# A hybrid encoder block: branch A's attention result split by halves of the tokens, and a third buffer for gate copies

## The chip, the cores and the metric

The kernel runs on one core of one Trainium2 chip. The metric is the device time of one execution in microseconds, as the median of several runs. Beside the runs there is one profiled execution, whose trace gives each instruction's start and length on the five engines: PE (TensorE, with its weight loads as PEld), DVE (VectorE), ACT (ScalarE), POOL (GpSimd) and SP (SyncE), which here issues the transfers (SPq).

## The reference, cut to what matters

The block takes x (1024 tokens of 1024 numbers, with 16 learned tokens put ahead), normalizes it, and projects it to the inputs of two attention branches and to two gates. Each branch gives 512 numbers for each token. They are merged, and a feed-forward part follows:

```python
y_a = differential_attention(...)        # 1024 x 512
y_b = windowed_gqa(...)                  # 1024 x 512
merged = sigmoid(ga) * (y_a @ w_ba) + sigmoid(gb) * (y_b @ w_bb)
h = h + merged @ w_o
h = h + (silu(n @ w_gate) * (n @ w_up)) @ w_down     # n = rms_norm(h, norm_ffn)
return rms_norm(h, norm_final)
```

All is in float32. [...] Making the two parts is called a split here: ACT copies the high part (`split`, L111), and DVE or POOL subtracts it from the number to get the low part (L112).

## The kernel before, in words

The work is laid out with features on the 128 partitions and tokens along the row. After the projections and branch B's attention comes branch A's attention; the projections to the gates (`gate_steps`, L535) are put between its matmuls, to fill PE. A gate's product of 512 tokens takes 24 matmuls into one PSUM bank; ACT copies the bank to a buffer `gate_stage` (L539), of which there are G_BUFS = 2, and SP sends the buffer to a tensor g_d in DRAM (L540). Two PSUM banks serve these products. The attention results go to DRAM too: yb_d, and ya_d (L653, one transfer for each head and each half of the tokens).

The merge (L755 to L811) has two loops. Both use weights in eight columns of 128 output features: `branch_w` (L522) loads one column (256 KB) and splits it, on ACT and POOL, into `wbhb` (branch B) or `wbha` (branch A), with WB_BUFS = 5 buffers for both. `branch_mm` (L529) makes the product of one column and one half of the tokens (512): 4 chunks of 128 features by three matmuls, so 12 matmuls into one of eight PSUM banks. A pass of `gated` (L775) loads the gate's half row (`gt`, L778, GT_BUFS = 4 buffers), takes its sigmoid on ACT (L779), and calls `branch_mm`.

- Branch B's loop (L786): for each column and half, DVE multiplies gate and product into `tb` (L790). Its operand `yb` is loaded from yb_d in four transfers of 512 KB ahead of the loop and split in eight pieces of 512 tokens on ACT and DVE (`load_y`, L760). The raw numbers lie in a part of `tb` that is not yet in use, and the weights of the first two columns as well.
- Branch A's loop (L801): the same with `ya`, whose pool is opened where `yb`'s was closed (L791, L792), so in the same memory. DVE multiplies (L805), POOL adds `tb` (L806), and the sum is split into `mT` on ACT and DVE (L807). From the ninth pass on, a chunk of w_out is loaded and split in each pass (`prep_wo`, L749). The order of the passes is (column, half): columns 0 to 3 with both halves each, then columns 4 to 7 with the first half, then with the second.

The matmuls that follow (`po`, L832) multiply `mT` by w_out: four blocks of 128 tokens at a time, the first half of the tokens first.

The raw numbers of `ya`, of the weights and of w_out lie in a ring of RING_RAW = 5 buffers of 4 KB per partition (`raw_tile`, L744). The order of PE's instructions is that of the program text in this part (L784). Those of the other engines and of SP are put in order by a scheduler when the kernel is built; each engine and SP then works through its list strictly in order, and an instruction that waits holds up all behind it. Pools that are closed give their memory to pools opened later; an instruction that writes such memory waits until its last use is over.

`mpool` (L795), opened after `yapool`, holds `mT`, the row of norm_ffn (`gffn`, L797) and the first weights of the feed-forward part (`first_f`, L798 and L871).

## Time and profile before

| | us |
|---|---|
| median of 3 runs | 1466.54 |
| lowest and highest run | 1465.86, 1470.17 |
| the profiled execution's own time | 1467.45 |
| its span, first to last instruction | 1465.7 |
| mean granted TensorE clock in it (share of full speed) | 0.997 |

A line of the timeline gives the start and the length in us, the engine, the line of the kernel, the operation, what it writes <- what it reads, and the count of instructions merged; in brackets stands the idle time of the engine just before it, and what ended that. A line of the view of waits gives engine, tile and line <- what it waited for: us in total, times, and the longest. A line of the view of windows gives from:to, the length, the busy time of the engines asked for, then the granted clock, the share of the 16 transfer engines that was busy, and GB/s. A line on a tile's instructions gives the count, then min/median/max in ns. A line on transfers gives the count, the size of one, and the median us from issue to landing.

### The profile page before, as it was taken

What the parts mean: (1) busy time and instruction counts of PE and PEld (TensorE: products, weight loads), DVE (VectorE), ACT (ScalarE), POOL (GpSimd) and SP (SyncE); (2) the same over time, 40 slices, a digit from 0 to 9 for tenths busy, and PEclk for the clock granted to TensorE, in tenths of its full rate; (3) what the DMA queues carried; (4) which work ended last, traced back from release to release, by engine and by line L of the source; (5) the groups of instructions that cost most, each with busy time, mean ns of one, the idle gap of its engine ahead of it and who ended that gap; (6) DMA issues with size and microseconds to landing.
All of it is one profiled execution on the core that took longest, in us unless ns stands there. A gap on an engine that the chain in (4) does not pass through costs nothing.

```text
span 1465.7 us, 21002 instructions
## 1 busy us (share of the span) xinstructions
PE 1439.6 (98%) x7353; PEld 1237.5 (84%) x7353; DVE 859.0 (59%) x1664; ACT 654.6 (45%) x1237; POOL 529.8 (36%) x502
## 2 busy tenths in 40 slices
PE   6999999999999999999999999999999999999998
PEld 6988989988898989877888878888888888888886
DVE  6356426528686868423613876555555554787667
ACT  5365436525455555445412744333333333444454
POOL 4143223313323232223822566454545442000444
PEclk9999999999999999999999999999999999999999
DMA  7334353272524251086531434333333323954443
GB/s 233 89 98 115 111 127 98 77 204 96 152 73 145 73 153 66 31 277 196 169 126 61 141 122 135 126 103 98 108 103 105 101 93 102 345 201 141 125 124 142
DMA packets 155577, 189.96 MB, mean 130 GB/s; under 512 B 16128, under 2 KB 101568, under 8 KB 155472
## 3 DMA queue, kind: packets, MB, share of 16 engines
q1 hardware_dynamic: 155472, 188.63, 40.9%
q8 instruction: 58, 0.95, 0.3%
q14 instruction: 47, 0.39, 0.1%
HBM read 128.09 MB, written 53.94 MB: 124 GB/s over the span
## 4 chain that ended last, share of the span: by engine, by line
PE 86%; POOL 4%; issue 4%; DMA 3%; ACT 1%; DVE 1%; SPq 1%; POOLq 0%; ACTq 0%; DVEq 0%
PE pg L1055 26%; PE pp_g L199 10%; PE pd L1149 8%; PE ppa L532 6%; PE po L832 6%; PE aps L588 4%; PE apy L630 3%; PE pp_va L199 3%; PE pp_qb L199 3%; PE pp_qa L199 3%; PE pp_ka L199 3%; POOL oa L112 3%; PE apt L617 2%; PE bpt L337 2%; PE bpy L343 2%
## 5 line engine op out<-in xcount | busy, mean ns | idle before, releaser
L1055 PE MATMUL pg<-t,wop 128*128 128x512 f32 x1056 | 242.9, 389 | 0.2 <-POOL wop L112 0.2
L1055 PEld LDWEIGHTS pg<-t,wop 128*128 128x128 f32 x1056 | 198.1, 188 | 41.7 <-POOL wop L112 0.6
L112 POOL TENSOR_TENSOR wop<-wf,wop 128x512 fp32r<-128x512 f32 x128 | 171.6, 1345 | 165.9 <-ACT wop L111 152.1
L1149 PE MATMUL pd<-ob,oa 128*128 128x512 f32 x924 | 210.2, 389 | 0.8 <-POOL oa L112 0.4
L1149 PEld LDWEIGHTS pd<-ob,oa 128*128 128x128 f32 x924 | 173.3, 188 | 37.6 <-POOL oa L112 0.8
L1055 PE MATMUL pg<-b,wop 128*128 128x512 f32 x792 | 184.0, 390 | 2.7 <-DVE c L1064 2.7
L1055 PEld LDWEIGHTS pg<-b,wop 128*128 128x128 f32 x792 | 148.3, 188 | 34.2 <-issue 2.4
L112 POOL TENSOR_TENSOR wl_c<-w_c,wh_c 128x1024 fp32r<-128x1024 f32 x31 | 74.9, 2418 | 155.2 <-ACT wh_c L111 144.8
L111 ACT ACTIVATE wop<-wf 128x512 fp32r<-128x512 f32 x128 | 80.2, 631 | 85.2 <-PE pg L1055 48.4
L599 ACT ACTIVATE as<-as,amn 128x1040 f32<-128x1040 f32 x64 | 74.5, 1165 | 72.7 <-DVE amn L594 72.7
L112 POOL TENSOR_TENSOR oa<-ra,oa 128x512 fp32r<-128x512 f32 x33 | 44.0, 1335 | 170.8 <-ACT oa L111 169.4
L199 PE MATMUL pp_g<-hT_hi,wh_c 128*128 128x512 f32 x256 | 101.4, 396 | 0.6 <-DMA g_d<-gate_stage 0.6
L199 PE MATMUL pp_g<-hT_hi,wl_c 128*128 128x512 f32 x256 | 100.9, 394 | 0.0
L199 PE MATMUL pp_g<-hT_lo,wh_c 128*128 128x512 f32 x256 | 100.9, 394 | 0.0
L111 ACT ACTIVATE oa<-ra 128x512 fp32r<-128x512 f32 x77 | 48.7, 632 | 107.7 <-PE pd L1149 50.2
L588 PE MATMUL aps<-ak,aq 128*128 128x352 f32 (+1 forms) x384 | 92.6, 326 | 0.0
L832 PE MATMUL po<-woh,mT 128*128 128x512 f32 x384 | 88.0, 390 | 0.0
L890 DVE TENSOR_TENSOR s<-wf,wf 128x512 f32<-128x512 f32 x22 | 26.8, 1217 | 103.9 <-DMA wf<-in_w_ff_gate_dram 56.2
L832 PEld LDWEIGHTS po<-woh,mT 128*128 128x128 f32 x384 | 71.9, 188 | 14.8
L588 PEld LDWEIGHTS aps<-ak,aq 128*128 128x128 f32 x384 | 69.6, 188 | 14.0
L594 DVE CUSTOM_DVE_ANT_0 as<-aps,dist,amn 128x352 f32<-128x352 f32 (+1 forms) x128 | 71.3, 564 | 10.4 <-PE aps L588 8.4
L324 POOL TENSOR_SCALAR bs<-bs,bdn 128x432 f32<-128x432 f32 (+1 forms) x64 | 37.0, 596 | 94.8 <-DVE bdn L322 81.4
(249 smaller groups left out, 2943.1 us busy)
## 6 DMA issues: line engine op xcount, KB each, us to landing
ra<-aop SPq DMA_DIRECT2D x77, 256.0 KB, 2.6
w_c<-in_w_in_dram SPq DMA_DIRECT2D x33, 512.0 KB, 4.0
wf<-in_w_ff_gate_dram SPq DMA_DIRECT2D x24, 512.0 KB, 3.8
wf<-in_w_ff_up_dram SPq DMA_DIRECT2D x24, 512.0 KB, 3.8
aop<-as SPq DMA_DIRECT2D x44, 256.0 KB, 2.1
aop<-c SPq DMA_DIRECT2D x33, 256.0 KB, 2.0
g_d<-gate_stage SPq DMA_DIRECT2D x32, 256.0 KB, 2.0
gt<-g_d SPq DMA_DIRECT2D x32, 256.0 KB, 3.4
```

Source lines behind the costliest of these rows:

```text
L111: nc.scalar.activation(hi, src, AF.Copy)
L112: lo_eng.tensor_tensor(lo, src, f32(hi), ALU.subtract)
L199: nc.tensor.matmul(ps[:, :n], a[:, c, :], b[:, c, at:at + n], start=(c == 0 and i == 0), stop=(c == DC - 1 and i == 2))
L324: nc.gpsimd.tensor_scalar(st[:, r, :W], st[:, r, :W], dn[:, r:r + 1], 1.0, ALU.mult, ALU.mult)
L532: nc.tensor.matmul(ps, w[:, a, j, :], src[j][:, b, tk], start=(j == 0 and n == 0), stop=(j == 3 and n == 2))
L588: nc.tensor.matmul(ps[:, :n], qs[m][:, t * P:(t + 1) * P], ks[m][:, vv, k0:k0 + n], start=(vv == 0), stop=(vv == 1))
L594: nc.vector.tensor_tensor_reduce(s[m][:, a:b], ps[:, a - k0:b - k0], far_by, slope, low, ALU.add, ALU.min, mn[:, m, i + j:i + j + 1])
L599: nc.scalar.activation(s[m][:, 0:L], s[m][:, 0:L], AF.Exp, bias=low, scale=-1.0, accum_out=dn[:, m:m + 1])
L630: nc.tensor.matmul(py[:, cols], v[:kp, a, k, :], at_[:kp, k, b, :], start=(k == 0 and j == 0), stop=(k == 8))
L832: nc.tensor.matmul(ps, mT[:, c, a, t * P:(t + 1) * P], wos[q, c][:, b], start=(c == 0 and n == 0), stop=(c == DC - 1 and n == 2))
L1055: nc.tensor.matmul(ps, op[:, x, c, :], b[:, y, c, :], start=(p in (1, 2, 5) and c == 0 and n == 0), stop=(p in (4, 2, 3) and c == 3 and n ...
L1149: nc.tensor.matmul(ps[u], oa[:, a, u * P:(u + 1) * P], ob[:, b, :], start=(p in (1, 2, 5) and j == 0 and k == 0), stop=(p in (2, 3, 4) and ...
```

## The change

Branch A's `ya` is no longer loaded as four tensors of 1024 tokens after branch B's loop. It is loaded and split by halves of the tokens. A half has four loads of 512 tokens (256 KB each) into two ring buffers (`load_ya`) and four splits on ACT and DVE (`split_ya`). The first half is loaded after branch B's second column, and one of its pieces is split in each of the passes of B's columns 2 to 5, into a pool of its own (`ya0pool`, 16 KB per partition) that is opened ahead of `ybpool`. The second half is loaded after B's sixth column and split into `yapool` once `ybpool` is closed. Branch A's passes are put in the order columns 0 to 3 with the first half, then with the second, then columns 4 to 7 likewise. `yb` is loaded as before, written out in place. G_BUFS goes from 2 to 3.

```diff
-G_BUFS = 2
+G_BUFS = 3
...
-                nc.tensor.matmul(ps, w[:, a, j, :], src[j][:, b, tk],
+                nc.tensor.matmul(ps, w[:, a, j, :], src(j, b, tk),
...
     tb = ypool.tile([P, DC, S], F32, name="tb")
+    ya0pool, close_ya0 = pool("ya0pool")
     ybpool, close_yb = pool("ybpool")
...
+    def load_ya(half):
+        for i in range(2):
+            raw_ya[half, i] = raw_tile(f"raw_ya{half}_{i}")
+            for k in range(2):
+                nc.sync.dma_start(raw_ya[half, i][:, k * 512:k * 512 + 512], ya_d[2 * i + k][:, half * 512:half * 512 + 512])
+
+    def split_ya(half, j, p):
+        ya_t[half, j] = p.tile([P, 2, 512], F32R, name=f"ya{half}_{j}")
+        split(ya_t[half, j][:, 0], ya_t[half, j][:, 1], raw_ya[half, j // 2][:, j % 2 * 512:j % 2 * 512 + 512], nc.vector)
+
+    def ya(j, b, tk):
+        return ya_t[tk.start // 512, j][:, b]
...
             nc.vector.tensor_tensor(tb[:, o, tk], gt, ps, ALU.mult)
+        if o in (1, 5):
+            load_ya(o // 4)
+        if 2 <= o < 6:
+            split_ya(0, o - 2, ya0pool)
     close_yb()
     yapool, close_ya = pool("yapool")
-    ya = load_y(yapool, ya_d, "ya", lambda j: raw_tile(f"raw_ya{j}"))
+    for j in range(4):
+        split_ya(1, j, yapool)
...
-    order_a = [(o, h) for o in range(4) for h in range(2)] + [(o, h) for h in range(2) for o in range(4, DC)]
+    order_a = [(o, h) for b in range(0, DC, 4) for h in range(2) for o in range(b, b + 4)]
...
     close_ya()
+    close_ya0()
     close_ypool()
```

More of the change, by code (lines that the diff above doesn't have):

```diff
@@ L755, in encoder_block, with yb @@
     tb = ypool.tile([P, DC, S], F32, name="tb")
+    ya0pool, close_ya0 = pool("ya0pool")
     ybpool, close_yb = pool("ybpool")
     first_w = [branch_w(ypool, o, w_bb, "b", tb[:, 2, o * 512:o * 512 + 512]) for o in range(2)]
-    def load_y(p, src, nme, raw_of):
-        ys, raws_y = [], []
-        for j in range(4):
-            raws_y.append(raw_of(j))
-            nc.sync.dma_start(raws_y[j], src[j])
-            ys.append(p.tile([P, 2, S], F32R, name=f"{nme}{j}"))
-            if j % 2:
-                for h in range(2):
-                    cols = slice(h * 512, h * 512 + 512)
-                    for k in (j - 1, j):
-                        split(ys[k][:, 0, cols], ys[k][:, 1, cols], raws_y[k][:, cols], nc.vector)
-        return ys
-    yb = load_y(ybpool, yb_d, "yb", lambda j: tb[:, 4 + j, :])
+    yb_t = []
+    for j in range(4):
+        nc.sync.dma_start(tb[:, 4 + j, :], yb_d[j])
+        yb_t.append(ybpool.tile([P, 2, S], F32R, name=f"yb{j}"))
+        if j % 2:
+            for h in range(2):
+                cols = slice(h * 512, h * 512 + 512)
+                for k in (j - 1, j):
+                    split(yb_t[k][:, 0, cols], yb_t[k][:, 1, cols], tb[:, 4 + k, cols], nc.vector)
+    def yb(j, b, tk):
+        return yb_t[j][:, b, tk]
+    ya_t, raw_ya = {}, {}
+    def load_ya(half):
[8 more added lines that the diff above has]
+        return ya_t[tk.start // 512, j][:, b]
     def gated(i, o, half, w, src):
@@ L790, in encoder_block @@
             nc.vector.tensor_tensor(tb[:, o, tk], gt, ps, ALU.mult)
+        if o in (1, 5):
+            load_ya(o // 4)
+        if 2 <= o < 6:
+            split_ya(0, o - 2, ya0pool)
     close_yb()
     yapool, close_ya = pool("yapool")
-    ya = load_y(yapool, ya_d, "ya", lambda j: raw_tile(f"raw_ya{j}"))
+    for j in range(4):
+        split_ya(1, j, yapool)
     mpool, close_mpool = pool("mpool", "right")
```

## Prediction

> **What bounds the kernel now.** I read the page first: which engine is full, and whose time the chain of work that ended last holds.

> ```profile
> PE 1439.6 (98%) x7353; PEld 1237.5 (84%) x7353; DVE 859.0 (59%) x1664; ACT 654.6 (45%) x1237; POOL 529.8 (36%) x502
> PE 86%; POOL 4%; issue 4%; DMA 3%; ACT 1%; DVE 1%; SPq 1%; POOLq 0%; ACTq 0%; DVEq 0%
> ```

> TensorE (PE) is busy 98% of the span. The change takes no matmul away, so it can gain only where PE stands still or runs slowly. The view of PE's waits gives the places:

> ```profile
> PE pg L1055 <- DVE c L1064: 2.7, 2, 2.0
> ...
> PE ppa L532 <- ACT ya L111: 1.7, 1, 1.7
> ...
> PE pp_g L199 <- DMA g_d<-gate_stage: 0.6, 1, 0.6
> PE ppa L532 <- DVE ya L112: 0.5, 2, 0.3
> PE ppa L532 <- DVE yb L112: 0.4, 2, 0.2
> ```

> The change touches the ya waits (the step from branch B's products to branch A's) and the gate_stage wait. The timeline of PE shows the first place:

> ```profile
> 641.54 41.55 PE L532 MATMUL ppa<-yb,wbhb 128*128 128x512 f32 x182 [0.23 <-DVE yb L112]
> 684.75 0.50 PE L532 MATMUL ppa<-ya,wbha 128*128 128x512 f32 x1 [1.66 <-ACT ya L111]
> 685.48 2.15 PE L532 MATMUL ppa<-ya,wbha 128*128 128x512 f32 x6 [0.22 <-DVE ya L112]
> 687.88 4.35 PE L532 MATMUL ppa<-ya,wbha 128*128 128x512 f32 x14 [0.26 <-DVE ya L112]
> ...
> L532 PE MATMUL ppa<-yb,wbhb x192: 388/389/499, 638.2 to 682.7; 128*128 128x512 f32 x192
> ...
> 730.84 9.46 PE L832 MATMUL po<-woh,mT 128*128 128x512 f32 x41
> ```

> PE runs out of branch B's work at 683.09 and gets A's piece by piece. The cause is in ACT and DVE at the same moment:

> ```profile
> 684.09 4.26 ACT L111 ACTIVATE ya<-raw_ya 128x512 fp32r<-128x512 f32 x8
> 684.73 4.91 DVE L112 TENSOR_TENSOR ya<-raw_ya,ya 128x512 fp32r<-128x512 f32 x8 [0.84 <-ACT ya L111]
> ```

> All eight splits of ya start only when B's last product is done, since ya lies in yb's space. And the windows, one microsecond each (PE busy, granted clock, DMA share, GB/s), show that PE pays twice:

> ```profile
> 685.00:686.00 1.00, 0.78 (x3) 1.00 0.80 242
> 686.00:687.00 1.00, 1.00 (x5) 0.72 0.88 263
> 687.00:688.00 1.00, 0.74 (x3) 0.50 0.85 279
> 688.00:689.00 1.00, 1.00 (x3) 0.50 0.84 258
> 689.00:690.00 1.00, 1.00 (x4) 0.58 0.86 256
> 690.00:691.00 1.00, 1.00 (x6) 1.00 0.69 178
> ```

> After the wait the clock is halved for about 3.4 us: 0.28 + 0.50 + 0.50 + 0.42 = 1.70 us lost beside the idle time.

> **Part 1: half of ya is ready before B ends.** B's 182 matmuls take 41.55 us. One lasts 0.39 (the median of 389 ns in the row above) and they overlap, so the spacing is (41.55 - 0.39)/181 = 0.2274 us. Without a wait A's first matmul starts at 641.54 + 182 x 0.2274 = 682.93, its 192 matmuls take 43.66, and the first po matmul comes at 726.59 instead of 730.84: **4.25 us**. The other way round: waits of 1.66 + 0.22 + 0.26 = 2.14, three broken overlaps of 0.39 - 0.23 = 0.16 each, and 1.70 of clock make 4.32. I take 4.25.

> What has to be ready in time? The first four A products use the first half's ya alone. It is split on ACT and DVE beside B's products, some 34 us before use. The second half's splits still wait for the end of B (about 683.1). By the changed program's order of instructions ACT has two gate sigmoids and a w_out split ahead of them; if those run to 685.4, the four ACT and four DVE splits end at about 685.4 + 4 x 0.53 + 0.8 = 688.3 (0.53 = 4.26/8, 0.61 = 4.91/8 for DVE, from the rows above). They are first needed after 48 matmuls, at 682.93 + 10.92 = 693.85. Slack 5.5 us, so cost nothing; with the cover gone it would be the same kind of wait as today's.

> **Part 2: what moves ahead in SP's and ACT's queues.** The four first-half loads of ya (256 KB each) take the place of branch B's weight loads for columns 2 to 4 in SP's order, and four ya splits stand before these weights' splits on ACT. This is the change's own danger, for PE asks for column 2 early in B.

> ```profile
> 638.35 2.08 SPq L524 DMA_DIRECT2D wbrb<-in_w_branch_b_dram  x3
> ...
> 642.15 1.33 SPq L524 DMA_DIRECT2D wbrb<-in_w_branch_b_dram  x2
> ...
> wbrb<-in_w_branch_b_dram SPq DMA_DIRECT2D x2, 256.0 KB, 4.9
> ...
> DMA to landing us min/median/max: 8.0/8.7/10.3
> ...
> 643.06 2.19 ACT L779 ACTIVATE gt<-gt 128x512 f32<-128x512 f32 x4
> ...
> 645.86 5.05 POOL L112 TENSOR_TENSOR wbhb<-wbrb,wbhb 128x512 fp32r<-128x512 f32 x4 [11.17 <-ACT wbhb L111]
> ```

> (The line of landings is that of the four 512 KB loads of raw_ya; the wbrb line that of the two loads issued from 642.15 on.) Three ya loads go out at 638.35; the fourth after the last gate copy at 642.15; column 2's weights at about 642.8. The position in the transfers is that of today's fifth wbrb, which landed after 4.9 us, so 647.7. ACT finishes four gates at 645.25, the fourth ya split (its load lands at about 647.0) by 647.6, column 2's high half at 648.3; POOL's low half takes 5.05/4 = 1.26, to 649.6. PE wants the high half after 48 matmuls of B, at 641.54 + 38 x 0.2274 = 650.18, the low half two matmuls later, 650.64. Slack about 1.0 us: **cost taken as 0**, since the nearest row by place and size is the 4.9. The bounds: nothing can be gained here (today PE does not wait for wbhb); with the slowest ya landing, 10.3, POOL ends at 655.0 and PE waits 4.4, with a halved clock after it 6.1. Columns 3 and 4 follow at POOL's 1.26 against 5.5 us of PE each.

> **Part 3: what moves into branch A's time.** norm_ffn's row and the two first weights of the feed-forward part (three transfers of 512 KB) move on SP from B's time to behind A's third gate load. The order of A's products becomes four columns by first half, then by second. A gate buffer comes free after multiply, add and split:

> ```profile
> L805 DVE TENSOR_TENSOR gt<-gt,ppa x16: 672/686/689, 690.2 to 734.8; 128x512 f32<-128x512 f32 x16
> L806 POOL TENSOR_TENSOR gt<-gt,tb x16: 1283/1292/1747, 691.0 to 735.7; 128x512 f32<-128x512 f32 x16
> L111 ACT ACTIVATE mT<-gt x16: 614/616/634, 693.8 to 737.3; 128x512 fp32r<-128x512 f32 x16
> L112 DVE TENSOR_TENSOR mT<-gt,mT x16: 686/1139/1676, 694.5 to 738.0; 128x512 fp32r<-128x512 f32 x16
> DMA to landing us min/median/max: 2.5/3.4/9.4
> ...
> 690.00:732.00 42.00, 42.00 (x187) 34.75 (x186) 25.05 (x28) 19.93 (x35) 36.27 (x26) 1.00 0.54 165
> ```

> 0.69 + 1.29 + 0.62 + 1.14 + 3.4 (gt's landing) + 0.63 (its sigmoid, alike) = 7.8 us, against four products of 12 x 0.2274 = 10.9 us per buffer; and eight PSUM banks let PE run eight products (21.8 us) ahead of a late multiply. The DMA share of 0.54 at 165 GB/s would become about 0.66 with 1.5 MB more in 42 us. So 0, and at most one late gate of 9.4 in place of 3.4 us, which the banks cover. POOL's 36.27 us are no more than before. po asks first for first-half tokens; A's last four products are second-half ones in both orders, so no new wait there. From po on, the order on every engine is that of before, so an earlier start is carried to the end.

> One more thing on Part 2. mT's low half takes DVE 686 to 1676 ns beside POOL, ya's 4.91/8 = 0.61 us with POOL idle; if one new ya split held POOL up for 0.61 us, column 2 would still keep 0.4 of its slack. [...]

> **Part 4: the third gate copy buffer.**

> ```profile
> 320.60 0.57 ACT L539 COPY gate_stage<-pp_g 128x512 f32<-128x512 f32 x1
> 331.79 0.58 ACT L539 COPY gate_stage<-pp_g 128x512 f32<-128x512 f32 x1 [10.62 <-DMA g_d<-gate_stage]
> ...
> 332.42 0.50 PE L199 MATMUL pp_g<-hT_hi,wh_c 128*128 128x512 f32 x1 [0.59 <-DMA g_d<-gate_stage]
> ```

> The third copy waits for the first one's transfer, which stands behind the attention loads, and PE then waits for a bank. With three buffers the third copy needs no transfer: **0.6 us**. The fourth waits to about 331.8 instead, when its bank isn't yet wanted. All later copies cost PE nothing today.

> **Sum.** 4.25 + 0.6 = 4.85 us off the profiled execution's own 1467.45 (span 1465.7 and 1.75 around it): **1462.6**. That execution lies 0.9 over the runs' median of 1466.54, whose runs go from 1465.86 to 1470.17. By the trace alone I cannot say that each run has the halved clock; a run without it would be at 1467.45 - 1.70 = 1465.75, about the lowest one. The changed kernel should have none, so I set its median a little under the sum: **1462.4**, 4.1 us or 0.28% under the median.

> **The rivals.**
> - *Late weights (the slower side).* Column 2's weights land after more than 5.9 us (648.7) and PE waits in B at 650. For: the DMA queue is full there and the slack is 1.0. Against: the row of 4.9. A landing of 7 us gives a wait of about 1 and 1463.6; the slowest landing gives 1462.6 + 6.1 = 1468.7. It ends above the median from a wait of 2.2 with the halved clock (3.9 together), a landing of about 8.1.
> - *The halved clock is not due to the wait and stays.* Then only 2.14 + 0.48 + 0.6 = 3.2 goes: 1464.2. For: the wait of 1.99 us for c is followed by no drop:

> ```profile
> 855.46 5.72 PE L1055 MATMUL pg<-b,wop 128*128 128x512 f32 x24 [1.99 <-DVE c L1064]
> ...
> 853.00:856.00 3.00, 1.01 (x6) 1.00 0.33 116
> 856.00:859.00 3.00, 3.00 (x15) 1.00 0.02 5
> ```

>   Against: that wait stood alone, ours has two more behind it, and the drop begins 1.7 us after its end (0.72 in the window from 686). [...]
> - *The split does not do it.* The second half, a weight or a gate is late inside A and PE waits at 693.9 instead: a wait of 2.1 with the clock gives the 4.25 back and leaves 1466.8.

> **Chances.** Faster by over 0.3% means under 1462.1, slower over 1470.9 (0.3%, 4.4 us, is about what a measurement of this kernel can tell from no change). Forecast 0.72: its own range 1461.2 to 1463.8 lies across 1462.1, because the median may or may not hold the halved clock, so 0.42 faster, 0.30 same. Late weights 0.14: 0.10 same, 0.04 slower, where columns 3 and 4 are late as well. Clock stays 0.08, same. Split does not do it 0.06: 0.05 same, 0.01 slower. Sum: **faster 0.42, same 0.53, slower 0.05**. Range 1460.5 to 1467.0: it takes in the late weights up to a wait of about 3 and the rival of the clock, and leaves out under 2 in 10.

> **What would show it.** Right: no PE wait for ya, first po matmul 48 us less 4.25 after B's end, no window under 1.00 there, ya's first splits on ACT between 645 and 648, no wait at pp_g near 332. Wrong: PE waiting for wbhb near 650, or for ya, wbha or a PSUM bank after 683; or the same clock drop without a wait.

## The result, and the profile after

| kernel | median, us | lowest to highest | runs | ratio to before [95% interval] |
|---|---|---|---|---|
| before | 1467.28 | 1465.72 to 1471.44 | 19 | |
| changed | 1464.08 | 1461.67 to 1468.95 | 19 | 0.9979 [0.9971, 0.9988] |
| changed, measured again beside experiments | 1465.80 | 1463.82 to 1468.37 | 11 | 0.9992 [0.9983, 1.0001] |

The change is worth 0.1 to 0.2%, some 1.5 to 3 us: under the 0.3% that counts as a difference here, and less than the 4.1 us of the forecast. The interval of the second measurement takes in 1, no change. The profiled execution of the changed kernel takes 1464.08 (span 1462.3) against 1467.45 (span 1465.7).

The waits of PE in the changed kernel: engine, tile and line <- what it waited for, us in total, times, longest.

```profile
PE pg L1076 <- DVE c L1085: 2.3, 2, 2.0
...
PE apt L617 <- DVE as L605: 0.7, 1, 0.7
PE ppa L532 <- POOL wbha L112: 0.7, 1, 0.7
```

The waits for ya, yb and the gate copy are gone. Two of 0.7 us are new: for the first softmax of branch A (`apt`, its transposes, <- `as`), and for a low half of branch A's weights (`wbha` <- POOL). PE's timeline of the merge:

```profile
638.60 43.75 PE L532 MATMUL ppa<-yb,wbhb 128*128 128x512 f32 x192
682.19 30.54 PE L532 MATMUL ppa<-ya,wbha 128*128 128x512 f32 x134
713.43 13.44 PE L532 MATMUL ppa<-ya,wbha 128*128 128x512 f32 x58 [0.70 <-POOL wbha L112]
726.71 33.48 PE L853 MATMUL po<-woh,mT 128*128 128x512 f32 x147
```

Counted from start to start, before against after:

| stretch | before | after | difference |
|---|---|---|---|
| start of branch B's products | 638.16 | 638.60 | +0.44 |
| branch B's products, to A's first | 682.93 - 638.16 = 44.77, without the ya wait | 43.59 | -1.18 |
| branch A's products and the waits ahead of and in them, to po | 730.84 - 682.93 = 47.91 | 44.52 | -3.39 |
| first po | 730.84 | 726.71 | -4.13 |

The -3.39 is the forecast 4.25 less the new wait of 0.70 and its broken overlap of 0.16. The -1.18 was not forecast at all. And 0.7 us of the 4.13 is lost later: a stretch at half clock costs 1.7, and by the two views of waits some 1.0 of shorter ones in the feed-forward part comes back. In windows of the changed kernel (PE's busy time, granted clock, DMA share, GB/s):

```profile
687.00:690.00 3.00, 3.00 (x15) 1.00 1.08 318
...
851.00:854.00 3.00, 3.00 (x8) 0.54 0.02 5
854.00:857.00 3.00, 3.00 (x14) 0.89 0.24 90
```

After B's end the clock stays at 1.00. But now it is halved behind the wait for `c` in the feed-forward part, near 850, where it was not in the profile of before.

### The profile page after: what moved, and what is told of

Same layout as the page of the kernel before. It is cut to its first block, busy times and chain, and to the rows that moved or that the text cites. A ratio compares the mean times of both kernels' runs of the same rounds, so it can differ in the third digit from the quotient of the medians.

```text
span 1462.3 us, 21013 instructions
## 1 busy us (share of the span) xinstructions
PE 1438.5 (98%) x7353; PEld 1238.7 (85%) x7353; DVE 854.0 (58%) x1664; ACT 656.2 (45%) x1237; POOL 532.1 (36%) x502
## 4 chain that ended last, share of the span: by engine, by line
PE 88%; POOL 4%; issue 4%; DVE 2%; DMA 2%; ACT 0%; SPq 0%; POOLq 0%; DVEq 0%; ACTq 0%
PE pg L1076 28%; PE pp_g L199 12%; PE pd L1170 8%; PE po L853 6%; PE aps L588 4%; PE ppa L532 4%; PE apy L630 3%; PE pp_qb L199 3%; PE pp_ka L199 3%; PE pp_va L199 3%; PE pp_qa L199 3%; POOL oa L112 3%; PE apt L617 2%; PE bpt L337 2%; PE bpy L343 2%
## 5 line engine op out<-in xcount | busy, mean ns | idle before, releaser
L112 POOL TENSOR_TENSOR wop<-wf,wop 128x512 fp32r<-128x512 f32 x128 | 173.6, 1360 | 164.6 <-ACT wop L111 150.8
L112 POOL TENSOR_TENSOR wl_c<-w_c,wh_c 128x1024 fp32r<-128x1024 f32 x31 | 74.9, 2417 | 155.1 <-ACT wh_c L111 144.8
L111 ACT ACTIVATE wop<-wf 128x512 fp32r<-128x512 f32 x128 | 80.3, 632 | 85.2 <-PE pg L1076 50.7
L599 ACT ACTIVATE as<-as,amn 128x1040 f32<-128x1040 f32 x64 | 74.5, 1165 | 72.8 <-DVE amn L594 72.8
L112 POOL TENSOR_TENSOR oa<-ra,oa 128x512 fp32r<-128x512 f32 x33 | 44.0, 1335 | 170.5 <-ACT oa L111 169.1
L199 PE MATMUL pp_g<-hT_hi,wh_c 128*128 128x512 f32 x256 | 101.3, 396 | 0.0
L199 PE MATMUL pp_g<-hT_lo,wh_c 128*128 128x512 f32 x256 | 100.9, 394 | 0.0
L199 PE MATMUL pp_g<-hT_hi,wl_c 128*128 128x512 f32 x256 | 100.9, 394 | 0.0
L111 ACT ACTIVATE oa<-ra 128x512 fp32r<-128x512 f32 x77 | 48.7, 632 | 107.3 <-PE pd L1170 50.3
L911 DVE TENSOR_TENSOR s<-wf,wf 128x512 f32<-128x512 f32 x22 | 18.7, 850 | 107.0 <-DMA wf<-in_w_ff_up_dram 52.6
## 6 DMA issues: line engine op xcount, KB each, us to landing
ra<-aop SPq DMA_DIRECT2D x77, 256.0 KB, 2.6
aop<-as SPq DMA_DIRECT2D x44, 256.0 KB, 2.1
aop<-c SPq DMA_DIRECT2D x33, 256.0 KB, 2.0
g_d<-gate_stage SPq DMA_DIRECT2D x32, 256.0 KB, 2.0
gt<-g_d SPq DMA_DIRECT2D x32, 256.0 KB, 3.3
```

What stands on the lines that cost most here:

```text
L111: nc.scalar.activation(hi, src, AF.Copy)
L112: lo_eng.tensor_tensor(lo, src, f32(hi), ALU.subtract)
L199: nc.tensor.matmul(ps[:, :n], a[:, c, :], b[:, c, at:at + n], start=(c == 0 and i == 0), stop=(c == DC - 1 and i == 2))
L599: nc.scalar.activation(s[m][:, 0:L], s[m][:, 0:L], AF.Exp, bias=low, scale=-1.0, accum_out=dn[:, m:m + 1])
```

## The experiments

Ten measurements of nine kernels, in three sets; the kernels of a set shared a chip and the runs of before. The first set is the third buffer alone, the split alone, the low halves on DVE and the splits after B's end; the second is the changed kernel again, the split alone a second time, the low halves on DVE with two buffers, and `yb` moved; the third is the old order and both halves early. Medians are best compared within a set.

| experiment | median, us | lowest to highest | ratio to before [95% interval] |
|---|---|---|---|
| third buffer alone | 1467.19 | 1464.21 to 1471.19 | 0.9999 [0.9987, 1.0012] |
| split alone | 1466.07 | 1462.59 to 1468.36 | 0.9993 [0.9982, 1.0003] |
| split alone, second time | 1466.39 | 1465.09 to 1468.14 | 0.9992 [0.9984, 1.0001] |
| changed, low weight halves on DVE | 1464.06 | 1462.96 to 1465.60 | 0.9977 [0.9967, 0.9986] |
| the same, two gate buffers | 1463.64 | 1462.97 to 1467.85 | 0.9978 [0.9969, 0.9987] |
| changed, splits after B's end | 1474.07 | 1472.05 to 1474.69 | 1.0040 [1.0026, 1.0054] |
| changed, old order of A's passes | 1466.14 | 1463.44 to 1469.41 | 0.9994 [0.9982, 1.0005] |
| changed, both halves of ya early | 1466.78 | 1464.36 to 1469.03 | 0.9992 [0.9983, 1.0002] |
| before, with yb moved | 1467.05 | 1465.56 to 1470.25 | 0.9997 [0.9988, 1.0007] |

### The third gate buffer alone

```diff
 # on the kernel before
-G_BUFS = 2
+G_BUFS = 3
```

> The kernel before with three gate copy buffers and nothing else. By the prediction's fourth part it gains 0.6 us (ratio 0.9996), PE's wait for the gate copy near 332 us being gone. By the theory read from the changed kernel's trace it gains 0.0: the wait near 332 goes, and PE waits about 0.7 us for the first transposes near 341 instead, because the first softmax on ACT stands behind a split whose weights land at about 334. At the merge: waits for ya of about 2.1 us in total as before; if the halved clock is tied to that wait alone, it is there again at about 686 us, if it depends on how the wait falls in a window of the clock's own, it may be there, at the wait for c near 855, at both or at neither.

Measured: 0.9999, with an interval of 0.9987 to 1.0012, which is too wide to tell the 0.6 us (0.04%) from nothing. PE's wait for the gate copy is gone. What is late next can be seen on ACT, in before:

```profile
331.79 0.58 ACT L539 COPY gate_stage<-pp_g 128x512 f32<-128x512 f32 x1 [10.62 <-DMA g_d<-gate_stage]
333.17 1.06 ACT L111 ACTIVATE wh_c<-w_c 128x1024 fp32r<-128x1024 f32 x1 [0.80 <-PE pp_g L199]
...
334.60 1.17 ACT L599 ACTIVATE as<-as,amn 128x1040 f32<-128x1040 f32 x1
```

and in the changed kernel:

```profile
325.79 0.59 ACT L539 COPY gate_stage<-pp_g 128x512 f32<-128x512 f32 x1 [4.20 <-PE pp_g L199]
334.03 1.06 ACT L111 ACTIVATE wh_c<-w_c 128x1024 fp32r<-128x1024 f32 x1 [7.65 <-DMA w_c<-in_w_in_dram]
...
335.46 1.17 ACT L599 ACTIVATE as<-as,amn 128x1040 f32<-128x1040 f32 x1
```

The copy comes 6 us sooner, and then ACT stands 7.65 us on the next instruction of its list, the split of the next gate weights, whose transfer has yet to land. Behind it stands the first softmax exponential (L599), which starts 0.86 us later than before, and PE's transposes of it (`apt`) wait. In SP's list that transfer is issued at 329.38, behind a gate send whose issue alone took 2.21 us:

```profile
327.07 2.21 SPq L540 DMA_DIRECT2D g_d<-gate_stage  x1
329.38 0.38 SPq L170 DMA_DIRECT2D w_c<-in_w_in_dram  x1
```

In the profile of this experiment the softmax (333.76) came in time, so the wait changes with the landing; there neither wait is left, and B's products start at 637.22, 0.94 us sooner than in before. Over six profiles with the split and three buffers PE waited 0.27 to 1.04 us there or, with the splits after B's end, not at all; over four with the split or the moved yb and two buffers it waited 0.2 to 1.2 us at `pp_g`. With the split, then, the buffer exchanges one wait for another of the same order. Whether a few tenths of a us are won by it is open.

### The split alone, and the low halves of the weights

The second kernel is the changed one with two gate buffers, measured twice; the third gives the low halves of branch A's weight columns 5 to 7 to DVE, and the fourth does that with two gate buffers.

```diff
 # the third and the fourth; the second and the fourth have G_BUFS = 2
-        split(wh[:, 0], wh[:, 1], w, nc.gpsimd)
+        split(wh[:, 0], wh[:, 1], w, nc.vector if nme == "a" and o >= 5 else nc.gpsimd)
```

> The changed kernel with two gate copy buffers. If the third buffer gives nothing, the time is that of the changed kernel (ratio to the kernel before 0.998); if it gives 0.6 us, it is 0.6 us over it (0.9984). The wait near 332 (0.6 us) should be back and that near 341 gone. At the merge: no wait for ya, a wait of 0.7 us for POOL's low half of branch A's last weights near 713. If the third buffer also made branch B's start free of waits (0.45 us less at 638), those waits are back here; if that was chance, they may be absent.

> The changed kernel, with the low halves of branch A's weight columns 5 to 7 made by DVE instead of POOL. If POOL's strict order (sums and w_out splits ahead of column 7's low half) makes PE's wait near 713, it goes, and branch A's 192 matmuls take 43.7 us in place of 44.5, 0.8 us less (ratio 0.9974 to the kernel before, within the scatter of the changed kernel's 0.998). If the wait comes from the weights' own load or from ACT, it stays at 0.5 to 0.7.

> The changed kernel with two gate buffers, measured beside the changed kernel itself. The profile of the first look gave the third buffer nothing (span 1461.2 without it, 1462.3 with it), its runs gave it 2 us (1466.1 without it, 1464.1 with it, though on another chip). If the profile is right, both medians lie within 1 us of each other here, both some 0.2% under the kernel before. If the runs are right, this kernel is 1.5 to 2 us slower than the changed kernel.

> The changed kernel with the low halves of branch A's weight columns 5 to 7 on DVE instead of POOL, and with two gate buffers instead of three. If the third buffer brings nothing, because the wait that it removes near 332 us is replaced by a later first softmax, this kernel is within 0.05% of the same kernel with three buffers, about 1464.1, and PE shows the 0.5 us wait for gate_stage near 332 or none, and no 0.7 to 0.9 us wait for the first softmax near 341. If the third buffer is worth the predicted 0.6 us beside the split, it is 0.6 us or more slower, about 1464.7 to 1466. Branch A's 192 products should take 43.5 to 43.7 us in both cases.

Measured: the split alone gains 0.07 and 0.08%, both times with an interval that touches 1. With the weights on DVE the gain is 0.23 and 0.22%, with three gate buffers and with two. So the third buffer is worth nothing that can be measured beside the split. And within a set the low halves on POOL cost 2.0 to 2.8 us: 1463.64 without them against 1466.39 (split alone) and 1465.80 (changed) in the second, 1464.06 against 1466.07 (split alone) in the first, with intervals that hardly overlap. Only the changed kernel's first measurement, in a set of its own, was as good (0.9979) with POOL. So the place where the rest of the gain can be lost is POOL. On the changed kernel's POOL, the stretch that ends the new wait:

```profile
706.21 1.74 POOL L826 TENSOR_TENSOR gt<-gt,tb 128x512 f32<-128x512 f32 x1
707.91 2.99 POOL L112 TENSOR_TENSOR woh<-wo,woh 128x512 fp32r<-128x512 f32 x2
710.86 1.29 POOL L826 TENSOR_TENSOR gt<-gt,tb 128x512 f32<-128x512 f32 x1
712.10 1.27 POOL L112 TENSOR_TENSOR wbha<-wbra,wbha 128x512 fp32r<-128x512 f32 x1
```

ACT has column 7's high half done at 706.94; POOL works through two sums and two splits of w_out, which nobody needs before 726, and only then makes the low half. PE wants it at 712.73. The stretch has no idle time on POOL, so any delay that reaches POOL earlier reaches PE. In the second measurement of the split alone, ACT and PE:

```profile
688.14 0.63 ACT L111 ACTIVATE woh<-wo 128x512 fp32r<-128x512 f32 x1 [2.67 <-DMA wo<-in_w_out_dram]
688.68 2.18 ACT L111 ACTIVATE ya<-raw_ya 128x512 fp32r<-128x512 f32 x4
```

```profile
684.00 30.54 PE L532 MATMUL ppa<-ya,wbha 128*128 128x512 f32 x134
717.13 13.44 PE L532 MATMUL ppa<-ya,wbha 128*128 128x512 f32 x58 [2.60 <-POOL wbha L112]
```

One chunk of w_out landed late. ACT, in order, had its split ahead of the second half of ya and of column 4's weights: 4.14 us after A's start, where the changed kernel's came 2.2 after it (684.41, A's start 682.19). POOL followed, 1.9 us later against A's start than in the changed kernel from column 4's low half on, and PE waited 2.60 instead of 0.70. The wait was 0.70, 0.74, 0.90 and 2.60 in the four profiles of the changed kernel and of the split alone. With the weights on DVE it is gone, and A's 192 products take the undisturbed time:

```profile
682.09 43.68 PE L532 MATMUL ppa<-ya,wbha 128*128 128x512 f32 x192
725.61 9.68 PE L853 MATMUL po<-woh,mT 128*128 128x512 f32 x42
```

This kernel, with either number of gate buffers, has the best time of its set.

### The splits after B's end, and the old order

The fifth kernel keeps the early loads but splits the first half only when branch B's loop is over; the sixth keeps all of the change but the order of A's passes.

```diff
 # fifth
-    ya0pool, close_ya0 = pool("ya0pool")
     ybpool, close_yb = pool("ybpool")
...
-        if 2 <= o < 6:
-            split_ya(0, o - 2, ya0pool)
     close_yb()
+    ya0pool, close_ya0 = pool("ya0pool")
     yapool, close_ya = pool("yapool")
+    for j in range(4):
+        split_ya(0, j, ya0pool)
 # sixth
-    order_a = [(o, h) for b in range(0, DC, 4) for h in range(2) for o in range(b, b + 4)]
+    order_a = [(o, h) for o in range(4) for h in range(2)] + [(o, h) for h in range(2) for o in range(4, DC)]
```

> The changed kernel with the first half of ya split into memory that branch B's operand holds until its end; loads by halves, order of the products and three buffers are kept. If the early split is what gains, PE waits for ya at 683 again, 2.1 us or somewhat less, since ACT and DVE still come only then (the first matmul 1.7 us late, then piece by piece), with the halved clock behind it in some executions: ratio about 0.9995 to 1.0005. If the earlier loads or the new order of the products gain, it keeps most of it: 0.998 and no wait over 0.5.

> The changed kernel with branch A's passes in the order of before (columns 0 to 3 with both halves each). Now the second half of ya is asked for by the second product, 12 matmuls (2.7 us) after branch B's end, and not by the fifth. In the changed kernel its first split on ACT begins 2.8 us after B's end and its first low half on DVE ends 0.6 + 0.6 us later. If the new order of passes is a needed part of the gain, PE waits 1 to 2 us for ya again, in two or three pieces, and the time is 1465 to 1467, near that of the kernel before. If the split alone carries the gain, the time is the changed kernel's, 1464 to 1466. The clock: the rule found in ten profiles (a window of a free-running grid of 3.413 us in which PE stands idle for 1.9 us or more is followed by one at half clock, one with under 1.85 us by none) should hold for every window here.

Measured: without the early splits PE waits 6.04 and 0.59 us for ya, and the time is 1474.07. The wait is larger than that of before because ACT's list there has the splits of ya behind that of a weight column, for whose load it stands 2.27 us more:

```profile
687.82 0.63 ACT L111 ACTIVATE wbha<-wbra 128x512 fp32r<-128x512 f32 x1 [2.27 <-DMA wbra<-in_w_branch_a_dram]
688.36 4.25 ACT L111 ACTIVATE ya<-raw_ya 128x512 fp32r<-128x512 f32 x8
```

Two windows at half clock follow, in which PE is busy for 1.78 and 3.41 us: by estimate half of that, 2.6 us, is lost. With the old order the wait is back too, at the second product:

```profile
682.30 2.88 PE L532 MATMUL ppa<-ya,wbha 128*128 128x512 f32 x12
686.33 0.51 PE L532 MATMUL ppa<-ya,wbha 128*128 128x512 f32 x1 [1.14 <-ACT ya L111]
687.71 42.46 PE L532 MATMUL ppa<-ya,wbha 128*128 128x512 f32 x179 [0.88 <-DVE ya L112]
730.01 5.38 PE L853 MATMUL po<-woh,mT 128*128 128x512 f32 x23
```

So the early splits and the order of passes are both needed if PE is not to wait for ya. By time only the splits are shown to be needed: the old order's 0.9994 (0.9982 to 1.0005) is not clear of the changed kernel's 0.9979 and 0.9992. The old order has its own merit, though: there POOL's low half of column 7 starts at 708.46 and not at 712.10, and there is no wait for wbha. It is the new order that puts it 3.6 us later on POOL: between the low halves of columns 4 and 7 POOL has seven sums there, and five in the old order as in before.

### Both halves early: the price of late weights

```diff
-        if o in (1, 5):
-            load_ya(o // 4)
+        if o == 1:
+            load_ya(0)
+            load_ya(1)
```

> The changed kernel with both halves of branch A's result loaded after branch B's second column: four more loads of 256 KB stand ahead of column 2's weights in SP's queue, and two more ring buffers stay taken until branch B's end. This prices the rival of the late weights. In the changed kernel column 2's high half starts on ACT at 646.8 and its low half is done about 1.0 us before PE wants it. If the transfers ahead set the landing (1 MB more at the 280 to 320 GB/s of the windows near there is 3 to 3.5 us), PE waits 2 to 3 us for wbhb near 650 and the time is 1466 to 1469. If there is more cover than the slack of 1.0 us says, there is no wait and the time is 1464 to 1466. The rule of the clock as for the other kernel: half clock only behind a grid window with 1.9 us or more of idle PE.

Measured: 1466.78, and in PE's timeline of branch B

```profile
639.86 11.08 PE L532 MATMUL ppa<-yb,wbhb 128*128 128x512 f32 x48
651.40 0.73 PE L532 MATMUL ppa<-yb,wbhb 128*128 128x512 f32 x2 [0.46 <-ACT wbhb L111]
652.76 32.49 PE L532 MATMUL ppa<-yb,wbhb 128*128 128x512 f32 x142 [0.62 <-POOL wbhb L112]
```

The wait is where it was expected, after 48 products, but 1.08 us and not 2 to 3. The mechanism of that rival is real; the size is a third to a half of the estimate from the transfers. ACT's split of column 2 starts at 650.72, 10.86 us after B's first product, where in the changed kernel it is 8.21 (646.81 - 638.60): it comes 2.65 later, and the slack takes up some 1.1 of that. The rest of the loss here is a wait of 2.03 us for column 7's low half, as above, with a stretch at half clock behind it.

### Before, with yb moved

```diff
 # on the kernel before; nothing uses the reserved space
+    hold0, close_hold0 = pool("hold0")
+    for j in range(4):
+        hold0.tile([P, 2, 512], F32R, name=f"hold0_{j}")
     ybpool, close_yb = pool("ybpool")
...
     close_yb()
+    close_hold0()
```

> The kernel before, with 16 KB per partition reserved and left unused below yb until branch B's loop ends, so that yb lies at the place that it has in the changed kernel; the transfers and their order are those of before. As a side effect, two of ya's four pieces lie in the reserved space and need not wait for branch B's end. If the place of yb is what brought its first load down from 6.9 to 5.8 us and took away PE's two waits of 0.2 us at the start of branch B, both go here too, and branch B's 192 products take about 43.6 us. If the cause is another part of the change, the first landing stays at 6.8 to 6.9 us, the two waits stay, and the products take about 44.1 to 44.8 us. The whole time isn't what is asked: between 1463 and 1467.

Measured: neither outcome. Landings of the four loads of yb, in before:

```profile
DMA to landing us min/median/max: 6.9/8.0/9.2
```

in the changed kernel:

```profile
DMA to landing us min/median/max: 5.8/6.9/8.1
```

and in this experiment:

```profile
DMA to landing us min/median/max: 6.4/7.5/8.7
```

PE has one of the two waits for yb left (0.22). Over all profiles, a first landing of 6.1 us or less goes with no wait and one of 6.4 or more with one or two. The kernels that open ya0pool ahead of ybpool had 4.5 to 6.1 us, but for one with 6.6; the three others, this experiment aside, had 6.8 to 6.9. What shortens it stays open.

### The changed kernel again

> The changed kernel as it is, beside the two others. About 1464 and a ratio of 0.998. The clock: either theory of the halved clock (a stretch of 3.41 us that follows each wait of about 2 us, or one that falls on such a wait only in some executions) leaves no stretch at the merge, for there is no wait of 2 us there; the first expects one at the wait for c near 851 us again, the second may show none.

Measured: 0.9992, with the wait for wbha at 0.74 us and the clock halved behind the wait for c again. The two theories of the clock were told apart by all twelve profiles together. In the records of the granted clock each halved stretch within PE's work lasts 3.41 us, in one kernel twice that, and all stretches of an execution lie on one grid of 3.413 us: in before a halved stretch starts at 686.43 and one behind PE's last work at 1461.26, 774.83 us or 227 times 3.4133 later; in the changed kernel two such stretches lie 178 times 3.4133 us apart. The grid lies differently in each execution: its first record stands 19.6 to 22.5 us after the start; what went before it is not known. Windows cut on that grid, in before:

```profile
683.02:686.43 3.41, 1.53 (x6) 1.00 0.40 127
686.43:689.84 3.41, 3.15 (x8) 0.50 0.82 250
...
853.69:857.10 3.41, 1.64 (x7) 1.00 0.09 29
857.10:860.51 3.41, 3.41 (x16) 1.00 0.20 77
```

in the changed kernel:

```profile
847.83:851.25 3.42, 1.40 (x6) 1.00 0.42 148
851.25:854.66 3.41, 3.41 (x9) 0.50 0.02 5
```

and, in the second measurement of the split alone, the 2.60 us of the wait for wbha, which fall across two windows, and the wait for c, which falls into one:

```profile
712.02:715.43 3.41, 2.51 (x12) 1.00 0.77 261
715.43:718.84 3.41, 1.71 (x7) 1.00 0.49 144
...
851.96:855.38 3.42, 1.43 (x6) 1.00 0.31 108
855.38:858.79 3.41, 3.41 (x9) 0.50 0.02 5
```

| idle PE in one grid window, us | next window |
|---|---|
| 3.42 (splits late), 2.03 (both early), 2.02 (old order), 2.02 (changed), 2.00 (changed, again), 1.99 (split, second time), 1.99 (splits late), 1.88 (before) | half clock |
| 1.88 (yb moved), 1.86 (old order), 1.77 (before), 1.70 (split, second time), and all smaller ones in windows that were themselves at full clock | full clock |

The table holds the waits inside the kernels, not their first 20 and last 10 us. What ten profiles had shown of this was on record before the last two kernels (old order, both early) were run, and their profiles agree. So in these twelve profiles every window in which PE was idle for 1.99 us or more of 3.41 was followed by one at half clock, whether PE was then busy or not, which cost 1.7 us where it was busy; of two with 1.88 one was. A wait of 2 us in one piece did it in some executions and not in others: the c wait, 2.0 us in all twelve, in 4 of 12.

## Why the prediction was right or wrong, point by point

- **What bounds the kernel, and the direction.** Right: 1464.08 and 1465.80 lie in the range and in the case "within 0.3%", though the forecast itself, 1462.4, is 1.7 us below the first measurement and 3.4 below the second. That the first came so near is in part luck: in the profile, the 1.18 us in branch B that nobody forecast stood against 0.86 lost at wbha and the 0.6 of the third buffer that did not show. And by the prediction's own signs one of being wrong came true: PE waited for wbha after 683.
- **Part 1, the boundary.** The mechanism is right and the trace pays it to the hundredth: 4.25 less the 0.86 of a new wait is the 3.39 measured. The second half's splits ended at 688.77 on DVE (forecast 688.3), needed at 693.1. What was mis-sized is one term, as a part of the median: the **1.70 us of the clock**. The sentence that failed is "The changed kernel should have none". It has the halved clock behind the c wait instead, and the kernel with the third buffer alone, whose merge is that of before, does not have it at the boundary. Going by the table above, both first waits, 683.09 to 685.48, 2.39 us from start to end, with the 1.88 idle us of before in them, must fall into one window, so by estimate, with the waits of this profile and a grid that lies anywhere with the same chance, (3.41 - 2.39)/3.41 = 0.3 of the executions of before pay it. Over the runs it is then worth about 0.5 us, not 1.7. The profile was one of the 0.3.
- **The rival of the clock.** Its claim, that the drop is not due to the wait, is wrong: in the third-buffer kernel waits of 1.48 + 0.23 + 0.55 lay across three windows (0.71, 1.06, 0.49 idle) and there was no drop; in the old-order kernel the waits put 2.02 us into one and there was. But the answer given to it, "that wait stood alone", is wrong too. The c wait of before put 1.77 us into one window by the chance of the grid. The row that spoke against counting the term in full stood in the prediction. That this rival's 1464.2 lies next to the measured 1464.08 is chance: the drop at the boundary went, and one elsewhere came.
- **Part 2, column 2's weights.** Right. The changed kernel's ACT and POOL:

```profile
644.43 2.18 ACT L111 ACTIVATE ya<-raw_ya 128x512 fp32r<-128x512 f32 x4
646.81 0.63 ACT L111 ACTIVATE wbhb<-wbrb 128x512 fp32r<-128x512 f32 x1 [0.20 <-DMA wbrb<-in_w_branch_b_dram]
```

```profile
647.52 5.57 POOL L112 TENSOR_TENSOR wbhb<-wbrb,wbhb 128x512 fp32r<-128x512 f32 x4 [12.52 <-ACT wbhb L111]
```

  The first of the four low halves is done by 648.9, PE wants it at 638.60 + 50 x 0.2274 = 649.97: about 1.1 us of slack, forecast 1.0. (The splits of ya began at 644.43, a little ahead of the 645 named.) That there is little more was shown by the kernel with both halves early.
- **Part 3, branch A's time.** Wrong: 0 forecast, 0.7 to 2.6 us measured. The step that failed is "POOL's 36.27 us are no more than before". It counts POOL's work and not its order and due time. POOL's low half of column 7 in before:

```profile
709.51 1.28 POOL L112 TENSOR_TENSOR wbha<-wbra,wbha 128x512 fp32r<-128x512 f32 x1
```

  It was done at 710.79 and PE came to it at about 717.65 (730.84 - 58 x 0.2274), so there were 6.9 us of slack. In the changed kernel PE comes at 712.73, 4.9 sooner, and POOL is done at 713.37, 2.6 later, about the time of the two sums more (1.29 each) that the new order of passes puts ahead; 6.9 is 0.6 less than 7.5, and PE waited 0.70. The third rival ("a weight or a gate is late inside A") had the right place and too small a chance, 0.06, because it was thought of as a replacement of the whole gain.
- **Part 4, the third buffer.** Not borne out: 0.6 forecast, and the runs, which can't resolve 0.6, show nothing. The wait went as forecast; what came next in ACT's list, a weight split whose load stands behind the gate sends on SP, was not asked for, and with the split PE waited up to 1.04 us there. In the two profiles branch A's first scores start 0.42 us later after the change (329.76 against 329.34) and B's products 0.44 later: between the two nothing was won. But the start of the scores alone ranges from 328.8 to 330.2 over the twelve profiles, and in that of the buffer alone 0.94 was won at B's start, so single profiles don't settle it.
- **Not forecast.** Branch B's 1.18 us, with the two waits of 0.22 and 0.23 for yb; its cause is open.

Together: 2.62 of waits and overlaps + 0.5 of clock + 0 to 1.2 in B - 0.9 to 2.8 for wbha = 0.3 to 3.4 us by estimate, against 1.5 and 3.2 measured.

## What to carry to other kernels

When a change makes one engine come earlier, list for each in-order engine what it must have ready by then, and subtract: the slack of a helper engine falls by the time that is won, however idle it is on average. Work that nobody needs yet (w_out here) should not stand ahead of work that is due, on ACT, POOL or SP alike. And a loss that hangs on where an execution falls on the clock's grid must be weighed by how often that happens before it enters a forecast of a median (here 1.7 us, by estimate in 0.3 of the executions of before).

## What the runs showed of the hardware

In before, the 128x512 matmuls of branch B, three to a chunk (high by high, high by low, low by high), followed each other every 0.2274 us at a granted clock of 1.00: 182 of them took 41.55 us, one 0.39.

```profile
684.56:687.98 3.42, 0.00 (x0) 1.00 0.46 152
687.98:691.39 3.41, 1.78 (x3) 0.50 0.08 23
691.39:694.80 3.41, 3.41 (x9) 0.50 0.90 287
```
